# Six one-bank PSUM tiles for attention, and one-bank tiles for its projections and gates

## The chip, the cores and the metric

The kernel runs on one core of a Trainium2 chip. The metric is device time in microseconds (us) of one execution, given as the median of several runs. A core has TensorE (in the profile PE for its matmuls, PEld for loading their weights), VectorE (DVE), ScalarE (ACT), GpSimd (POOL) and SyncE (SP), which here issues most DMAs. TensorE writes its results to PSUM, and VectorE and ScalarE copy them to SBUF. PSUM is used here in units of one bank: 128 partitions by 512 float32 values, the most that one matmul of this kernel writes. There are eight banks.

## The reference, cut to what matters

One layer of a bidirectional encoder over 1024 tokens of width 1024. Its first part has two branches that share one input projection: windowed attention with grouped heads, and a state-space scan (SSD). Each branch is projected, gated by a sigmoid and merged; then come cross-attention and an MLP. The change concerns the windowed attention, and the gates that are computed beside it:

```python
proj = h @ w_in[i]
q = proj[..., :OFF_K].reshape(b, l, 16, 64)        # 16 heads of 64
k = proj[..., OFF_K:OFF_V].reshape(b, l, 4, 64)    # 4 key heads, each for 4 query heads
v = proj[..., OFF_V:OFF_Z].reshape(b, l, 4, 64)
gate_a, gate_b = ...                                # 1024 columns each
# per block of 128 queries: keys of this block and of both neighbours
s = einsum('bnqgrd,bnkgd->bngrqk', qb, kw) * 64 ** -0.5 + bias   # ALiBi, banded
m = max(max(s), sink); p = exp(s - m); denom = sum(p) + exp(sink - m)
o = einsum('bngrqk,bnkgd->bnqgrd', p / denom, vw)
merged = sigmoid(gate_a) * (attn @ w_attn_branch) + sigmoid(gate_b) * (ssd @ w_ssd_branch)
```

## The kernel before, in words

Phases follow one another: norms and small projections, the SSD scan (`ssd_phase`), attention (`attn_phase`), the merge (`merge_phase`), cross-attention and the MLP. In the SSD phase and from the merge on, the order of TensorE's instructions is the order in which they are written. In `attn_phase` it isn't: there the scheduler of the build orders every engine's instructions, by their place in the program among those that it holds to be ready, and that order is then fixed. So TensorE's order interleaves the steps below. In all phases waits are placed by data and by buffers: a tile of a pool with `bufs=n` takes the place of an earlier one, and waits until that one has been read.

Large products are made in three passes of high and low parts (`mm3`, lines 85, 89 and 90), so `gemm_fm` makes 24 matmuls for one block of 128 features by 512 tokens: 8 slices of the contraction by 3. The activations `kx.hT` (tile name kt) lie in two token halves. Weights are loaded by SP, split into whi (ACT, line 66) and wlo (POOL, line 69).

Before the change PSUM is shared out as follows in the SSD phase and in attention: the pool `pg` holds two tiles of two banks ([128, 1024], tag g), and the pool `pp` four tiles of one bank (tag p). The merge opens a pool of eight one-bank tiles in their place (line 1647).

Attention runs over four key heads kv. For each:

- For every second kv, keys of two heads are projected to a two-bank tile (`kps`, 48 matmuls), then copied to kh (ACT, lines 694 and 695) and to the rests kl (DVE, lines 696 and 697). The tags kh and kl have two buffers each, so keys of heads 2 and 3 need the buffers of heads 0 and 1.
- For the first kv, values are projected for all heads (`v_part`, tile vp, in the pool `pp`).
- Queries of two heads at a time are projected to a two-bank tile (`qps`, 48 matmuls; twice for each kv). ACT copies one head's half of the partitions (line 714), DVE computes the rest to the other half (line 715). The tag q has six buffers, of which a kv uses four.
- `scores(qb)` for each of eight query blocks: for each of four heads two matmuls to a one-bank tile sps (lines 732 and 733), then one DVE instruction that adds the bias, stores the sum to t and takes its minimum, nm (line 734). Then DVE and ACT compute the exponentials of t (line 740) and the denominators, and POOL scales t (line 745). The tag t4 has three buffers.
- `values(qb)`: for each of two or three key blocks, four transposes of t to a one-bank tile pt (line 755), copied by ACT to ph (line 758) and by DVE to the rest pl (line 759); then pairs of matmuls with ph and pl add up in a one-bank tile op (lines 764 and 765). ACT copies it in two halves, oa and ob (lines 768 and 769), POOL adds them, and SP stores the sum.
- The program makes `scores` two blocks ahead of `values`.
- After the last block of a kv come the gates of `ATT_GATES[kv]`: none, 11, 12, and 13 and 14. A gate is a two-bank tile gps of 48 matmuls, two ACT copies through a tanh (line 347), and two stores.

Since the order is by readiness, the matmuls of gates and of the next kv's keys and queries fill in between those of scores and values.

Of the kernel before, what the change touches and what calls it, by code (L numbers as in the profile page):

```python
# [7 lines left out]
F32 = mybir.dt.float32  # L8
F32R = mybir.dt.float32r
I32 = mybir.dt.int32  # L10
AF = mybir.ActivationFunctionType
ALU = mybir.AluOpType
AX = mybir.AxisListType
PSUM = bass.MemoryType.PSUM
DRAM = bass.MemoryType.DRAM

P = 128
S = 1024
# [74 lines left out]
def act_pair(act, k, sl=slice(None)):  # L93
    t = act[k // 4]
    return t[:, k % 4, 0, sl], t[:, k % 4, 1, sl]
# [6 lines left out]
def wsplit(w, nk=NK):  # L102
    hi = w[0].rearrange("p (k c) -> p k c", k=nk)
    lo = w[1].rearrange("p (k c) -> p k c", k=nk)
    return [(hi[:, k], lo[:, k]) for k in range(nk)]


def gemm_fm(kx, ps, w, act, first=True, last=True):

    ws = wsplit(w)  # L110
    for k in range(NK):
        mm3(kx, ps, ws[k], act_pair(act, k), first and k == 0, last and k == NK - 1)
# [224 lines left out]
def gate_block(kx, ins, dr, m, pool=None, pin=False):  # L337
    nc = kx.nc
    w = wload(kx, ins["wg"][m])
    ps = kx.pg.tile([P, S], F32, tag="g", name="gps")  # L340
    if pin:
        pin_next_matmul(kx)
    for h in range(2):
        gemm_fm(kx, ps[:, h * 512:(h + 1) * 512], w, kx.hT[h])
    gt = (pool or kx.tabp).tile([P, 2, 512], F32, tag="tab", bufs=1, name="gt")
    for h in range(2):
        nc.scalar.activation(gt[:, h], ps[:, h * 512:(h + 1) * 512], AF.Tanh, scale=0.5)
        (nc.sync if m in (7, 8) else nc.scalar).dma_start(dr.gt[m][h], gt[:, h])


def pin_next_matmul(kx):
    kx.pin = True
# [296 lines left out]
def attn_phase(kx, ins, dr):  # L649
    nc, tc = kx.nc, kx.tc  # L650
    V, A, G, PE = nc.vector, nc.scalar, nc.gpsimd, nc.tensor
    with tc.tile_pool(name="p2", bufs=1) as ap, tc.tile_pool(name="p2r", bufs=1, side="right") as aq:
# [30 lines left out]
        kd = {}  # L683
        for kv in range(4):
            if kv % 2 == 0:
                w = wload(kx, ins["wk"][kv // 2])
                ps = kx.pg.tile([P, S], F32, tag="g", name="kps")
                for h in range(2):
                    gemm_fm(kx, ps[:, h * 512:(h + 1) * 512], w, kx.hT[h])
                for s in range(2):  # L690
                    kh = aq.tile([P, S], F32R, tag="kh", bufs=2, name="kh")
                    kl = aq.tile([P, S], F32R, tag="kl", bufs=2, name="kl")
                    own, oth = slice(64 * s, 64 * s + 64), slice(64 - 64 * s, 128 - 64 * s)
                    A.activation(kh[own], ps[own], AF.Copy)
                    A.activation(kh[oth], ps[own], AF.Copy)
                    V.tensor_tensor(kl[own], ps[own], kh[own].bitcast(F32), ALU.subtract)
                    V.tensor_tensor(kl[oth], ps[own], kh[own].bitcast(F32), ALU.subtract)
                    kd[kv + s] = (kh, kl)
            if kv == 0:
                v_part()  # L700
            qs, bias = [], []
# [3 lines left out]
                bias.append(bt)  # L705
            for i in range(2):
                w = wload(kx, ins["wq"][2 * kv + i])
                ps = kx.pg.tile([P, S], F32, tag="g", name="qps")
                for h in range(2):
                    gemm_fm(kx, ps[:, h * 512:(h + 1) * 512], w, kx.hT[h])  # L710
                for s in range(2):
                    q = aq.tile([P, S], F32R, tag="q", bufs=6, name="q")
                    own, oth = slice(64 * s, 64 * s + 64), slice(64 - 64 * s, 128 - 64 * s)
                    A.activation(q[own], ps[own], AF.Copy, scale=-0.125)
                    V.scalar_tensor_tensor(q[oth], ps[own], -0.125, q[own].bitcast(F32), ALU.mult, ALU.subtract)
                    qs.append((q, own))
            kh, kl = kd[kv]
            def scores(qb):
                kb0, kb1 = max(qb - 1, 0), min(qb + 2, NT)
# [60 lines left out]
            for m in ATT_GATES[kv]:  # L780
                gate_block(kx, ins, dr, m)
# [821 lines left out]
@with_exitstack  # L1603
def hybrid_encoder(ctx, tc, ins, out, dbg=None):
    nc = tc.nc
    kx = Ctx()
    kx.nc, kx.tc = nc, tc
    kx.pin = False
    kx.w_bufs = 3
    kx.raw_bufs = 2  # L1610
    kx.cp = ctx.enter_context(tc.tile_pool(name="const", bufs=1))
    kx.wp = ctx.enter_context(tc.tile_pool(name="w", bufs=1))
    kx.mp = ctx.enter_context(tc.tile_pool(name="m", bufs=1))
    psum = ExitStack()
    kx.pg = psum.enter_context(tc.tile_pool(name="pg", bufs=2, space=PSUM))
    kx.pp = psum.enter_context(tc.tile_pool(name="pp", bufs=4, space=PSUM))
    dp = ctx.enter_context(tc.tile_pool(name="dram", bufs=1, space=DRAM))
    dr = Ctx()
    dr.cs = dp.tile([P, 512], F32, name="d_cs")
    dr.dec = dp.tile([P, 4], F32, name="d_dec")  # L1620
    dr.kx = dp.tile([P, 1024], F32, name="d_kx")
    dr.vx = dp.tile([P, 1024], F32, name="d_vx")
    dr.at = [[dp.tile([P, 4, 512], F32, name=f"d_at{k}_{h}") for h in range(2)] for k in range(2)]
    dr.y = [dp.tile([P, S], F32, name=f"d_y{k}") for k in range(16)]
    dr.gt = [[dp.tile([P, 512], F32, name=f"d_gt{k}_{h}") for h in range(2)] for k in range(16)]
    dr.x1 = [dp.tile([P, D], F32, name=f"d_x{k}") for k in range(4)]
    dr.u = [dp.tile([P, 1024], F32, name=f"d_u{k}") for k in range(32)]
    kx.dbg = dbg
    consts(kx)
    with tc.tile_pool(name="dtc", bufs=1) as dtc:  # L1630
        kx.coef = dtc.tile([P, 2, 4, 2, 32], F32, name="coef")
        kx.ebias = dtc.tile([P, 2, 4, 2, 32], F32, name="ebias")
        kx.ecs = dtc.tile([P, 2, 4, 2, 32], F32, name="ecs")
        kx.dec = dtc.tile([P, P, 4], F32, name="dec")
        with tc.tile_pool(name="conv", bufs=1) as kx.conv_pool:
            phase0(kx, ins, dr)
            ssd_phase(kx, ins, dr)
    with tc.tile_pool(name="tabp", bufs=1) as kx.tabp:
        attn_phase(kx, ins, dr)
        x1_low = ExitStack()  # L1640

        def x1_open():
            high = ctx.enter_context(tc.tile_pool(name="x1b", bufs=1, side="right", reuse_waits="tile"))
            return [x1_low.enter_context(tc.tile_pool(name="x1a", bufs=1, side="right", reuse_waits="tile")), high]

        psum.close()
        kx.pp = ctx.enter_context(tc.tile_pool(name="p8", bufs=8, space=PSUM, reuse_waits="tile"))
        h2T = merge_phase(kx, ins, dr, x1_open)
        ok, grow = cross_phase(kx, ins, dr, *h2T)
        with tc.manual_schedule(engines={mybir.EngineType.PE}):  # L1650
            down_phase(kx, ins, dr, up_phase(kx, ins, dr, ok, grow, x1_low), out)
    kx.dr = dr
    return kx
# [73 lines left out]
```

## Time and profile before

| | us |
|---|---|
| median of 3 runs | 2354.52 (2348.69 to 2355.77) |
| profiled execution | 2358.81 |
| its span, first to last instruction | 2357.0 |
| TensorE busy with matmuls | 2316.2 (98%) |
| TensorE busy loading weights | 1937.7 (82%) |
| DVE, ACT, POOL busy | 1623.7, 1155.2, 956.8 |

The granted TensorE clock was 0.997 of full speed. The keys' first matmul in attention starts at 909.65 us of the span, and the merge's first at 1236.91. In rows of the profile, L732 is line 732 of the kernel; `sps<-kh,q` is what an instruction writes and reads; x128 counts instructions. In a list of instructions the two first numbers are the start and the duration in us, and brackets hold the idle time of the engine before it and what ended it. A matmul's duration includes its way through the array, so durations of following matmuls overlap; how fast they follow is read from their starts.

### The profile page before, as it was taken

The page shows a single profiled execution, that of the slowest core. Times are in us where ns is not written, and L with a number is a line of the kernel's source. Part 1 is how long each engine was busy: PE and PEld are TensorE (multiplying, and loading weights), DVE is VectorE, ACT ScalarE, POOL GpSimd, SP SyncE. Part 2 cuts the span into 40 slices and gives each one's busy share as a digit, 9 for nine tenths or more (in the row PEclk, how much of TensorE's full clock was granted, in tenths as well). Part 3 has the DMA queues.
Part 4 walks back from the last instruction along what each step waited for, and adds up shares of the span by engine and source line. Part 5 has one row for each costly group of instructions (what it writes and reads, how often), then busy time and mean ns, then how long its engine had stood idle before and what let it go on. Part 6 is the DMA issues. An engine that isn't in the chain of part 4 may idle for free.

```text
span 2357.0 us, 32504 instructions
## 1 busy us (share of the span) xinstructions
PE 2316.2 (98%) x11876; PEld 1937.7 (82%) x11876; DVE 1623.7 (69%) x2539; ACT 1155.2 (49%) x2462; POOL 956.8 (41%) x891
## 2 busy tenths in 40 slices
PE   9999999999999999999999999999999999999998
PEld 7888898988889898877777888788977887788887
DVE  4777766677766664474568887975585456689984
ACT  4455655555555564586775442345453333134341
POOL 2355647565574653454540014215475444200010
PEclk9999999999999999999999999999999999999999
DMA  6223323232232322111136256202353345722301
GB/s 221 90 76 96 103 77 112 77 108 81 90 113 72 121 83 79 41 36 59 37 95 227 72 182 234 75 18 81 115 169 129 107 130 178 290 81 86 120 27 72
DMA packets 150036, 251.04 MB, mean 107 GB/s; under 512 B 11250, under 2 KB 86130, under 8 KB 149876
## 3 DMA queue, kind: packets, MB, share of 16 engines
q1 hardware_dynamic: 79264, 210.67, 26.3%
q10 hardware_dynamic: 70612, 38.29, 5.8%
q8 instruction: 94, 1.54, 0.3%
q14 instruction: 66, 0.54, 0.1%
HBM read 201.47 MB, written 47.45 MB: 106 GB/s over the span
## 4 chain that ended last, share of the span: by engine, by line
PE 79%; DVE 9%; DMA 3%; ACT 3%; issue 3%; POOL 2%; SPq 0%; POOLq 0%; ACTq 0%; DVEq 0%
PE dps L1497 10%; PE mps L1497 8%; PE pb L1292 6%; PE cps L90 4%; PE cps L85 4%; PE cps L89 4%; PE pc L1292 3%; PE zp L85 3%; PE zp L90 3%; PE zp L89 3%; PE cb L572 2%; PE yo L576 2%; PE gps L85 2%; PE gps L89 2%; PE gps L90 2%
## 5 line engine op out<-in xcount | busy, mean ns | idle before, releaser
L69 POOL TENSOR_TENSOR wlo<-raw,whi 128x1024 fp32r<-128x1024 f32 x104 | 255.6, 2458 | 408.2 <-ACT whi L66 379.9
L1497 PE MATMUL mps<-kt 128*128 128x512 f32 x1008 | 232.2, 391 | 4.9 <-DVE kt L1449 4.9
L1448 ACT ACTIVATE kt<-row 128x512 fp32r<-128x512 f32 x264 | 144.3, 619 | 187.1 <-PE dps L1497 83.0
L1497 PE MATMUL dps<-kt 128*128 128x512 f32 x1008 | 228.6, 389 | 0.0
L1497 PEld LDWEIGHTS mps<-kt 128*128 128x128 f32 x1008 | 189.7, 189 | 46.3 <-DVE kt L1449 7.0
L1497 PEld LDWEIGHTS dps<-kt 128*128 128x128 f32 x1008 | 189.2, 188 | 39.3
L85 PE MATMUL cps<-kt,whi 128*128 128x512 f32 x512 | 215.0, 420 | 0.0
L90 PE MATMUL cps<-kt,wlo 128*128 128x512 f32 x512 | 200.0, 391 | 0.0
L89 PE MATMUL cps<-kt,whi 128*128 128x512 f32 x512 | 199.3, 389 | 0.0
L66 ACT ACTIVATE whi<-raw 128x1024 fp32r<-128x1024 f32 x104 | 109.5, 1054 | 183.1 <-DMA raw<-in_wa_dram 42.1
L1449 DVE TENSOR_TENSOR kt<-row,kt 128x512 fp32r<-128x512 f32 x264 | 172.2, 700 | 3.8 <-ACT kt L1448 3.7
L124 POOL TENSOR_TENSOR rr<-rv,mhalf 128x1 f32<-128x1 f32 (+1 forms) x50 | 35.0, 701 | 235.8 <-DVE rv L122 229.8
L514 POOL TENSOR_TENSOR xl<-xs,xh 128x512 fp32r<-128x512 f32 (+1 forms) x64 | 86.3, 1350 | 103.5 <-ACT xh L513 79.0
L1238 POOL TENSOR_TENSOR wop<-w,wop 128x512 fp32r<-128x512 f32 x64 | 85.4, 1338 | 87.8 <-ACT wop L1237 79.1
L89 PEld LDWEIGHTS cps<-kt,whi 128*128 128x128 f32 x512 | 96.3, 188 | 25.4 <-issue 6.7
L85 PEld LDWEIGHTS cps<-kt,whi 128*128 128x128 f32 x512 | 96.3, 188 | 24.9 <-issue 6.0
L90 PEld LDWEIGHTS cps<-kt,wlo 128*128 128x128 f32 x512 | 96.1, 188 | 20.7
L550 ACT ACTIVATE eb<-rows,ebias 128x128 f32<-128x128 f32 x256 | 89.1, 392 | 35.4 <-POOL rows L542 35.4
L549 ACT ACTIVATE ef<-rows,ebias 128x128 f32<-128x128 f32 x256 | 90.5, 393 | 30.3 <-PE cb L572 27.8
L1177 POOL TENSOR_TENSOR wd<-row,wd 128x1024 fp32r<-128x1024 f32 x4 | 11.2, 2801 | 228.4 <-ACT wd L1176 228.4
L85 PE MATMUL gps<-kt,whi 128*128 128x512 f32 x240 | 102.2, 426 | 0.0
L745 POOL TENSOR_SCALAR t<-t,den 128x384 f32<-128x384 f32 (+1 forms) x128 | 69.2, 560 | 80.4 <-DVE den L743 68.5
(377 smaller groups left out, 6586.4 us busy)
## 6 DMA issues: line engine op xcount, KB each, us to landing
rows<-d_cs ACTq DMA_DIRECT2D x128, 256.0 KB, 4.0
raw<-in_wssd_dram SPq DMA_DIRECT2D x48, 512.0 KB, 3.8
raw<-in_wup_dram SPq DMA_DIRECT2D x40, 512.0 KB, 3.8
d_u<-c SPq DMA_DIRECT2D x64, 256.0 KB, 2.3
row<-in_wdn_dram SPq DMA_DIRECT2D x28, 512.0 KB, 6.7
row<-d_u SPq DMA_DIRECT2D x28, 512.0 KB, 6.7
x<-in_x_dram SPq DMA_DIRECT2D x16, 512.0 KB, 6.4
raw<-in_wg_dram SPq DMA_DIRECT2D x16, 512.0 KB, 3.7
```

The costliest lines, as they stand in the source:

```text
L66: steps = [nc.scalar.activation(hi, raw, AF.Copy)]
L69: steps.append((eng or nc.gpsimd).tensor_tensor(lo, raw, hi.bitcast(F32), ALU.subtract))
L85: i = mm(out, l[0], r[0], start=first, stop=False)
L89: mm(out, l[0], r[1], start=False, stop=False)
L90: mm(out, l[1], r[0], start=False, stop=last)
L514: G.tensor_tensor(xl[:, lo:hi], xf[:, lo:hi], xh[:, lo:hi].bitcast(F32), ALU.subtract)
L549: A.activation(ef[:, h], rows[:, 0, h], AF.Exp, bias=kx.ebias[:, b, j, 0, o:o + 1])
L550: A.activation(eb[:, h], rows[:, 1, h], AF.Exp, bias=kx.ebias[:, b, j, 1, o:o + 1])
L1292: self.kx.nc.tensor.matmul(ps, w[:, i, ks], act[:, k, j], start=start and k == 0 and m == 0, stop=k == 3 and m == 2, skip_group_check=True)
L1448: nc.scalar.activation(t[:, j, 0], src, AF.Copy)
L1449: nc.vector.tensor_tensor(t[:, j, 1], src, t[:, j, 0].bitcast(F32), ALU.subtract)
L1497: self.kx.nc.tensor.matmul(ps[t], lt[:, k, x, ts], rt[:, k, y], start=n in (1, 2, 5) and k == 0 and m == 0, stop=k == 3 and m == 2, skip_g ...
```

## The change

After the SSD phase the PSUM pools are closed, and two new ones are opened for attention: `pg2` with two tiles of one bank and `pp6` with six tiles of one bank. Both are opened with `reuse_waits="tile"`: a tile waits only for those users of the old pools that used its own bank. Scores, transposes, outputs and the value projection then take their tiles from six in place of four. Projections of keys and queries and the gates of this phase are made in halves of 512 tokens, each in a one-bank tile of its own, and each half is copied when its own matmuls are done. The copies of keys and queries are twice as many, each half as wide; those of gates are as many and as wide as before. No matmul is added or removed, and no DMA.

```diff
 def gate_block(kx, ins, dr, m, pool=None, pin=False):
...
-    ps = kx.pg.tile([P, S], F32, tag="g", name="gps")
...
-    for h in range(2):
-        gemm_fm(kx, ps[:, h * 512:(h + 1) * 512], w, kx.hT[h])
     gt = (pool or kx.tabp).tile([P, 2, 512], F32, tag="tab", bufs=1, name="gt")
     for h in range(2):
-        nc.scalar.activation(gt[:, h], ps[:, h * 512:(h + 1) * 512], AF.Tanh, scale=0.5)
+        ps = kx.pg.tile([P, 512], F32, tag="g", name="gps")
+        gemm_fm(kx, ps, w, kx.hT[h])
+        nc.scalar.activation(gt[:, h], ps, AF.Tanh, scale=0.5)
...
@@ attn_phase, keys
-                ps = kx.pg.tile([P, S], F32, tag="g", name="kps")
+                for s in range(2):
+                    kd[kv + s] = [aq.tile([P, S], F32R, tag=n, bufs=2, name=n) for n in ("kh", "kl")]
                 for h in range(2):
-                    gemm_fm(kx, ps[:, h * 512:(h + 1) * 512], w, kx.hT[h])
-                for s in range(2):
-                    kh = aq.tile([P, S], F32R, tag="kh", bufs=2, name="kh")
-                    kl = aq.tile([P, S], F32R, tag="kl", bufs=2, name="kl")
...
+                    ps = kx.pg.tile([P, 512], F32, tag="g", name="kps")
+                    gemm_fm(kx, ps, w, kx.hT[h])
+                    hs = slice(h * 512, (h + 1) * 512)
+                    for s in range(2):
+                        kh, kl = (t[:, hs] for t in kd[kv + s])
...
@@ attn_phase, queries
-                ps = kx.pg.tile([P, S], F32, tag="g", name="qps")
+                q2 = [aq.tile([P, S], F32R, tag="q", bufs=6, name="q") for _ in range(2)]
                 for h in range(2):
-                    gemm_fm(kx, ps[:, h * 512:(h + 1) * 512], w, kx.hT[h])
-                for s in range(2):
-                    q = aq.tile([P, S], F32R, tag="q", bufs=6, name="q")
...
+                    ps = kx.pg.tile([P, 512], F32, tag="g", name="qps")
+                    gemm_fm(kx, ps, w, kx.hT[h])
+                    for s in range(2):
+                        q = q2[s][:, h * 512:(h + 1) * 512]
...
+                qs += [(q2[s], slice(64 * s, 64 * s + 64)) for s in range(2)]
...
@@ hybrid_encoder, after ssd_phase
+    psum.close()
+    kx.pg = psum.enter_context(tc.tile_pool(name="pg2", bufs=2, space=PSUM, reuse_waits="tile"))
+    kx.pp = psum.enter_context(tc.tile_pool(name="pp6", bufs=6, space=PSUM, reuse_waits="tile"))
```

More of the change, by code (lines that the diff above doesn't have):

```diff
@@ L686, in attn_phase @@
                 w = wload(kx, ins["wk"][kv // 2])
-                ps = kx.pg.tile([P, S], F32, tag="g", name="kps")
+                for s in range(2):
+                    kd[kv + s] = [aq.tile([P, S], F32R, tag=n, bufs=2, name=n) for n in ("kh", "kl")]
                 for h in range(2):
-                    gemm_fm(kx, ps[:, h * 512:(h + 1) * 512], w, kx.hT[h])
-                for s in range(2):
-                    kh = aq.tile([P, S], F32R, tag="kh", bufs=2, name="kh")
-                    kl = aq.tile([P, S], F32R, tag="kl", bufs=2, name="kl")
[L693 to L698, printed above, removed]
+                    ps = kx.pg.tile([P, 512], F32, tag="g", name="kps")
[3 more added lines that the diff above has]
+                        kh, kl = (t[:, hs] for t in kd[kv + s])
+                        own, oth = slice(64 * s, 64 * s + 64), slice(64 - 64 * s, 128 - 64 * s)
+                        A.activation(kh[own], ps[own], AF.Copy)
+                        A.activation(kh[oth], ps[own], AF.Copy)
+                        V.tensor_tensor(kl[own], ps[own], kh[own].bitcast(F32), ALU.subtract)
+                        V.tensor_tensor(kl[oth], ps[own], kh[own].bitcast(F32), ALU.subtract)
             if kv == 0:
@@ L707, in attn_phase @@
                 w = wload(kx, ins["wq"][2 * kv + i])
-                ps = kx.pg.tile([P, S], F32, tag="g", name="qps")
+                q2 = [aq.tile([P, S], F32R, tag="q", bufs=6, name="q") for _ in range(2)]
                 for h in range(2):
-                    gemm_fm(kx, ps[:, h * 512:(h + 1) * 512], w, kx.hT[h])
-                for s in range(2):
-                    q = aq.tile([P, S], F32R, tag="q", bufs=6, name="q")
[L713 to L716, printed above, removed]
+                    ps = kx.pg.tile([P, 512], F32, tag="g", name="qps")
+                    gemm_fm(kx, ps, w, kx.hT[h])
+                    for s in range(2):
+                        q = q2[s][:, h * 512:(h + 1) * 512]
+                        own, oth = slice(64 * s, 64 * s + 64), slice(64 - 64 * s, 128 - 64 * s)
+                        A.activation(q[own], ps[own], AF.Copy, scale=-0.125)
+                        V.scalar_tensor_tensor(q[oth], ps[own], -0.125, q[own].bitcast(F32), ALU.mult, ALU.subtract)
+                qs += [(q2[s], slice(64 * s, 64 * s + 64)) for s in range(2)]
             kh, kl = kd[kv]
```

## The prediction

> **What bounds the kernel now.** I read the page's busy shares first, then cut the attention phase (909.65 to 1236.91 us) into stages, then read who waits for whom there, and last one steady stage in order of time.
>
> ```profile
> PE 2316.2 (98%) x11876; PEld 1937.7 (82%) x11876; DVE 1623.7 (69%) x2539; ACT 1155.2 (49%) x2462; POOL 956.8 (41%) x891
> ```
>
> TensorE is the bound, but 98% is matmul time with overlaps: it doesn't show the gaps. So I compare starts with the spacing of undisturbed matmuls. Next: stretches, with busy us (and instructions) of PE, PEld, DVE, ACT, POOL; the third row holds the matmuls and copies of qps alone.
>
> ```profile
> 1055.53:1061.73 6.20, 6.11 (x33) 4.72 (x33) 4.79 (x16) 5.22 (x16) 3.55 (x5) 1.00 0.10 24
> 992.00:1000.00 8.00, 8.00 (x43) 6.10 (x42) 6.55 (x18) 7.92 (x21) 5.53 (x9) 1.00 0.08 18
> 1085.40:1107.30 21.90, 21.84 (x96) 17.85 (x96) 2.44 (x2) 2.04 (x2) 1.00 0.19 61
> ```
>
> The third row is TensorE alone with a projection: 21.90/96 = 0.228 us for a 512-column matmul. The first is one steady attention stage (scores of one query block, values of an earlier one), 6.20 us long, in which no engine is full: ACT 5.22, DVE 4.79. Now the timeline of TensorE, weight loads, ACT and DVE around that stage.
>
> ```profile
> 1144.92 1.47 PE L755 MATMUL pt<-ident,t 128*128 128x128 f32 x12
> 1146.15 0.48 PE L90 MATMUL qps<-kt,wlo 128*128 128x512 f32 x1
> 1054.16 0.19 PEld L732 LDWEIGHTS sps<-kh,q 128*128 128x128 f32 x1 [0.39 <-DVE nm L734]
> 1055.53 0.52 PE L755 MATMUL pt<-ident,t 128*128 128x128 f32 x3
> 1057.13 0.60 PE L755 MATMUL pt<-ident,t 128*128 128x128 f32 x4
> 1057.33 1.28 DVE L759 TENSOR_TENSOR pl<-pt,ph 128x512 fp32r<-128x512 f32 x2
> 1057.46 0.59 ACT L768 ACTIVATE oa<-op 64x512 f32<-64x512 f32 x1
> 1058.06 0.50 PE L764 MATMUL op<-ph,vhl 128*128 128x512 f32 x1
> 1058.07 0.60 ACT L769 ACTIVATE ob<-op 64x512 f32<-64x512 f32 x1
> 1059.09 0.34 PE L732 MATMUL sps<-kh,q 128*128 128x384 f32 x1
> 1059.26 0.34 PE L733 MATMUL sps<-kl,q 128*128 128x384 f32 x1
> 1059.75 0.56 DVE L734 CUSTOM_DVE_ANT_0 t<-sps,bias 128x384 f32<-128x384 f32 x1 [1.15 <-PE sps L733]
> 1062.17 0.66 DVE L759 TENSOR_TENSOR pl<-pt,ph 128x512 fp32r<-128x512 f32 x1
> ```
>
> Spacings: a transpose (1146.15 - 1144.92)/12 = 0.103 us, a score matmul 1059.26 - 1059.09 = 0.17. The stage's 33 matmuls are 12 transposes, 8 scores, 6 for the output and so 7 of a projection or gate that fills in: 12 x 0.103 + 8 x 0.17 + 13 x 0.228 = 5.56 us. TensorE thus loses 6.20 - 5.56 = **0.64 us per stage**, 20.5 us over 32 stages (4 key heads x 8 blocks).
>
> Why the stage isn't shorter: count the four PSUM banks that sps, pt and op share. The third transpose bank is written at 1057.13 and read last by DVE until 1062.83: 5.7 us. An output bank is opened at 1058.06, so the one before it a stage earlier, at 1051.86, and that one is copied from 1057.46 to 1058.67: 6.8 us. The first two transpose banks are written from 1055.53 and read until 1058.61, each open some 2.5 us; four scores take some 1.2 us each (1059.09 to the end of the reduction at 1060.31). Together 5.7 + 6.8 + 5.0 + 4.8 = 22.3 bank-us, of 4 x 6.20 = 24.8: the four banks are 90% taken. The third score's weight load at 1054.16 waits for the reduction of an earlier score, and DVE sits idle 1.15 us for scores that have no bank. The weight loads' waits in the whole phase (total us, times, longest):
>
> ```profile
> PEld sps L732 <- DVE nm L734: 7.2, 23, 0.4
> PEld op L764 <- ACT ph L758: 6.9, 15, 0.7
> PEld pt L755 <- POOL t L745: 5.2, 16, 0.5
> PEld op L764 <- DVE pl L759: 4.7, 12, 0.5
> PEld op L765 <- DVE pl L759: 4.4, 12, 1.0
> PEld pt L755 <- issue: 3.7, 11, 0.6
> PEld sps L732 <- DVE q L715: 2.2, 6, 0.6
> PEld sps L732 <- ACT ob L769: 1.7, 3, 0.6
> PEld mps L85 <- ACT gt L347: 1.2, 1, 1.2
> ```
>
> Rows 1 and 8 are waits for a bank. I count rows 3 and 6 so too: the transposes follow the scores directly, and start when a reduction frees a bank; this is inferred. That makes 7.2 + 5.2 + 3.7 + 1.7 = 17.8. Waits for data are 6.9 + 4.7 + 4.4 = 16.0, and 2.2 are for a projection's copy. In all 36.0.
>
> **The change, part by part.**
>
> *Six banks for sps, pt, op instead of four.* The need of 22.3 bank-us becomes 22.3/6 = 3.7 us per stage and no longer binds; next in line are TensorE's 5.56 and ACT's 5.22. Of the 20.5 us lost, the bank waits' share is 17.8/36.0: **-10.1 us**. Ends: 0 (every wait comes back as another) and -20.5 (all waits go). I take the share, since only those waits have the removed cause.
>
> *Waits for data.* A shorter stage leaves ACT and DVE less slack, and the output matmuls wait for both already (16.0). I add **+1.5**, near the lower end of 0 to +10.1, since DVE's 1.15 us of idle time per stage covers the first of it.
>
> *Projections in two one-bank halves.* The matmuls stay as many. The copies of q and k double in number at half the width:
>
> ```profile
> L714 ACT ACTIVATE q<-qps 64x1024 fp32r<-64x1024 f32 x16 | 16.3, 1019 | 6.9 <-DVE q L715 6.8
> L768 ACT ACTIVATE oa<-op 64x512 f32<-64x512 f32 x32 | 18.8, 587 | 14.9 <-PE op L765 14.8
> L715 DVE SCALAR_TENSOR_TENSOR q<-qps,q 64x1024 fp32r<-64x1024 f32 x16 | 19.6, 1222 | 20.7 <-ACT q L714 20.4
> L759 DVE TENSOR_TENSOR pl<-pt,ph 128x512 fp32r<-128x512 f32 x88 | 57.2, 678 | 19.5 <-ACT ph L758 19.4
> L696 DVE TENSOR_TENSOR kl<-kps,kh 64x1024 fp32r<-64x1024 f32 x4 | 4.9, 1222 | 11.4 <-ACT kh L695 11.4
> ```
> ```profile
> L694 ACT ACTIVATE kh<-kps x4: 1001/1022/1023, 923.3 to 1091.5; 64x1024 fp32r<-64x1024 f32 x4
> ```
>
> ACT: 16 q copies and 8 of k (two lines of 4) grow from about 1020 to 2 x 587 = 1174 ns: 24 x 0.154 = 3.7 us. DVE: 24 x (2 x 0.678 - 1.222) = 3.2 us. On the path I put **0**: ACT is at 5.22 of 6.20 and, in the dense stretch, at 2.04 of 21.90 with q copies. Without that cover it is the 3.7, the upper end; the stretch 992 to 1000 (ACT 7.92 of 8) shows that cover can fail. In return the first half is copied while the second is multiplied, and scores of early blocks need only the first half: the 2.2 of waits for q go, by the same share 20.5 x 2.2/36.0 = **-1.2** (0 to -2.2). Here a rule speaks against the change: the Trainium skill's "Perfetto Trace Analysis", section "Optimizing Scalar/DVE Operations", says that each instruction on these engines pays a fixed data-access overhead, and that fewer, larger ones help where the engine is saturated. By its PSUM figures (about 51 ns on ScalarE, 125 on DVE) the estimate would be 24 x 51 = 1.2 and 24 x 125 = 3.0 us; the trace has 154 and 134 ns each, and the sum goes by the trace.
>
> *The gates* copy each half as it is done; the copies are as many and as wide as before. The last gate and the start of the phase:
>
> ```profile
> 1235.77 1.08 ACT L347 ACTIVATE gt<-gps 128x512 f32<-128x512 f32 x2 [1.06 <-PE gps L90]
> 1236.91 0.50 PE L85 MATMUL mps<-kt,whi 128*128 128x512 f32 x1 [0.89 <-ACT gt L347]
> 909.65 0.58 PE L85 MATMUL kps<-kt,whi 128*128 128x512 f32 x1
> 909.70 1.08 ACT L450 ACTIVATE gt<-gps 128x512 f32<-128x512 f32 x2
> 914.30 0.33 PE L606 MATMUL yt<-ident,yz 128*128 128x128 f32 x1 [0.86 <-ACT yz L598]
> ```
>
> At the end the merge's first matmul idles 0.89 us for both copies of the gate; the first half's bank will be free long before: **-0.9** (0 to -0.9). The stores of the gates stay on their queues; no transfer is added or moved.
>
> *The new pools ahead of attention.* Tiles wait per bank, not for the old pools as a whole. The first key projection starts at 909.65; if its bank was the previous gate's, it waits until 910.78: **+1.1**. At best 0. At worst the whole old pool must drain, and the key matmuls that now fill until the last transposes at 914.30 move behind them: +4.6. I take the wait for one bank, since that is what the pools declare.
>
> **Sum:** -10.1 + 1.5 + 0 - 1.2 - 0.9 + 1.1 = -9.6 us. It stands against this execution's 2358.8 (span 2357.0 and 1.8 around it): 2349.2. The median of the three runs is 2354.5, 4.3 lower, so I forecast **2345** as the median after. About 0.3% (7.1 us) is what a measurement of this kernel can tell from no change.
>
> **Rivals.**
>
> *Waits for data re-form (no change).* The instructions of each engine stand in a fixed order; if output matmuls wait for ph and pl as long as scores waited for banks, the 10.1 come back: -1.2 - 0.9 + 1.1 = -1.0, 2353.5. For it: 16.0 of 36.0 are such waits already. Against: DVE's 1.15 us idle is caused by banks. A measured case on this side, from the Trainium skill's "TensorE: Matmul & The Clock Gate", section "HAM oscillation — how this bites in real kernels": a matmul kernel gained nothing further from double-buffered PSUM. No run here shows it, and here the banks are 90% taken.
>
> *ACT is the bound (no change).* If ACT's 5.22 with its order sets the stage, the 10.1 don't come and the 3.7 lie on the path: +3.7 + 1.1 - 0.9 = +3.9, 2358.4. This is what the rule on larger instructions would give. For it: 7.92 of 8 us; against it: 16% idle in the steady stage.
>
> *DVE takes scores first (slower).* With banks free, scores of the next block come sooner, and their reductions (0.56 + 0.08 us each) may be queued ahead of the pl that the output waits for. Two of them ahead cost 1.28 per stage, less the 0.32 won (10.1/32): +0.96 in half of the stages, -0.32 in the rest: 16 x 0.64 = +10.2, 2365. From a delay of 0.32 us per stage the change loses. Against it: DVE is at 4.79 of 6.20.
>
> *The filling matmuls run dry (slower).* Two one-bank tiles hold 48 finished matmuls where two double tiles held 96. The second head's k copies wait for k buffers that the scores hold to the end of the stretch below. Its matmuls, first of the key tile, then of the gate:
>
> ```profile
> 1026.90:1069.20 42.30, 5.78 (x18) 3.15 (x19) 0.00 (x0) 0.00 (x0) 1.00 0.14 42
> 1026.90:1069.20 42.30, 14.89 (x48) 8.75 (x48) 1.09 (x2) 1.00 0.14 42
> ```
>
> 66 were used, and 96 can now be issued before both banks are stuck: 30 x 0.228 = 6.8 us to spare. If the order uses them up early, a stage loses its 7 x 0.228 = 1.6 us; ten such stages are 16, less the 9.6: +6.4, 2361. It decides from six stages on.
>
> **How the numbers follow.** Forecast 0.60, waits re-form 0.14, ACT 0.08, DVE 0.11, fillers 0.07. So faster 0.60, same 0.22, slower 0.18. The likeliest alone runs from 2334 (all 20.5 lost us won: -20.5 - 0.9 + 1.1 = -20.3) to 2347. The range is 2333 to 2361: it takes in both cases of no change, reaches to the fillers' price, and leaves out DVE's and half of the fillers'.
>
> **What would show it.** Right: the wait of sps for nm is near nothing, the steady stage near 5.8 us, DVE's idle time before its first reduction gone, spacings unchanged. Wrong: the waits of op for pl or ph above 16 us by the same amount; ACT full in steady stages; stages without projection matmuls; a gap between 909 and 915.

## The result, and the profile after

The changed kernel takes 2348.4 us (median of 22 runs, 2345.4 to 2353.2), the kernel before 2352.3 us (22 runs, 2348.1 to 2357.9): ratio 0.9985 with a 95% interval of 0.9980 to 0.9991. A second set of runs gave 0.9980 (0.9972 to 0.9989). So it is faster, but by 3.9 us instead of the forecast 9.6, which lies inside the 0.3% that the prediction called no change.

To compare the attention phase I use its length from the first matmul of kps to the first of mps. Every kernel below issues the same matmuls in it; at their undisturbed spacings they take 294.4 us (294.6 with 0.228, 0.174, 0.120 and 0.103 us for the 848, 192, 256 and 360 matmuls of 512, 384, 256 and 128 columns; differences between kernels don't hang on this figure). What the phase takes beyond that is called **lost time** of TensorE. In two executions of the change the phase took 322.72 and 322.70 us, so it repeats better than whole executions, which spread over 8 to 10 us; the kernel before and the same with its pools reopened differ more, 327.26 and 326.08. The timeline rows of the two matmuls that bound the phase after:

```profile
908.61 0.50 PE L85 MATMUL kps<-kt,whi 128*128 128x512 f32 x1 [0.83 <-ACT gt L449]
...
1231.32 0.39 PE L85 MATMUL mps<-kt,whi 128*128 128x512 f32 x1
```

The phase is 1231.32 - 908.61 = 322.71 us, before 1236.91 - 909.65 = 327.26: it lost 28.3 instead of 32.9 us. The weight loads' waits in the phase (total us, times, longest) changed like this:

```profile
PEld op L765 <- ACT ph L759: 8.8, 19, 0.9
PEld pt L756 <- POOL t L746: 6.2, 20, 0.6
PEld op L766 <- DVE pl L760: 5.6, 12, 1.4
PEld sps L733 <- DVE nm L735: 3.2, 7, 1.2
PEld qps L85 <- issue: 1.8, 1, 1.8
PEld kps L85 <- ACT gt L449: 1.2, 1, 1.2
```

The wait of scores for a bank (sps for nm) fell from 7.2 to 3.2, the waits for q and for ob are gone, and the outputs' waits for ph and pl fell from 16.0 to 14.4. The transposes' wait for t, which POOL scales, rose from 5.2 to 6.2. DVE's own waits, the first row before, the others after:

```profile
DVE t L734 <- PE sps L733: 50.6, 49, 6.3
```
```profile
DVE den L743 <- ACT t L741: 29.4, 19, 3.4
DVE t L735 <- PE sps L734: 13.6, 11, 3.0
```

DVE now rarely waits for scores (13.6 us instead of 50.6). It waits for ACT instead: 29.4 us for the exponentials in front of den (16.3 before), and 40.9 in front of its part of q (20.4 before). What became of the stages is seen in the last key head, by the copies of its first and its sixth output, before and after:

```profile
1195.98 0.60 ACT L769 ACTIVATE ob<-op 64x512 f32<-64x512 f32 x1
...
1229.57 0.59 ACT L769 ACTIVATE ob<-op 64x512 f32<-64x512 f32 x1
```
```profile
1189.85 0.60 ACT L770 ACTIVATE ob<-op 64x512 f32<-64x512 f32 x1
...
1218.66 0.59 ACT L770 ACTIVATE ob<-op 64x512 f32<-64x512 f32 x1
```

The first five stages last (1229.57 - 1195.98)/5 = 6.7 us before and (1218.66 - 1189.85)/5 = 5.8 after, and the last output is copied at 1224.57 instead of 1237.35, 12.8 us earlier. But the merge starts only 5.6 us earlier: between 1224.60 and 1231.30 TensorE is busy without a gap, with gate matmuls that used to fill the stages. **A shorter stage is no gain by itself. TensorE's work only moves, and the gain is the gaps that close.**

### The profile page after: what moved, and what is told of

It is laid out like the page before. It is cut to its first block, busy times and chain, and to the rows that moved or that the text cites. A ratio compares the mean times of both kernels' runs of the same rounds, so it can differ in the third digit from the quotient of the medians.

```text
span 2345.7 us, 32548 instructions
## 1 busy us (share of the span) xinstructions
PE 2307.1 (98%) x11876; PEld 1941.4 (83%) x11876; DVE 1620.7 (69%) x2563; ACT 1157.8 (49%) x2486; POOL 959.2 (41%) x891
## 4 chain that ended last, share of the span: by engine, by line
PE 81%; DVE 8%; ACT 4%; issue 3%; POOL 3%; DMA 1%; POOLq 0%; ACTq 0%; DVEq 0%
PE dps L1498 10%; PE mps L1498 9%; PE pb L1293 6%; PE cps L90 5%; PE cps L85 5%; PE cps L89 4%; PE pc L1293 3%; PE zp L85 2%; PE zp L90 2%; PE zp L89 2%; PE cb L571 2%; PE yo L575 2%; PE gps L89 2%; PE gps L85 2%; PE gps L90 2%
## 5 line engine op out<-in xcount | busy, mean ns | idle before, releaser
L89 PEld LDWEIGHTS cps<-kt,whi 128*128 128x128 f32 x512 | 96.3, 188 | 25.3 <-issue 6.7
L548 ACT ACTIVATE ef<-rows,ebias 128x128 f32<-128x128 f32 x256 | 90.6, 393 | 33.9 <-PE cb L571 31.7
L1178 POOL TENSOR_TENSOR wd<-row,wd 128x1024 fp32r<-128x1024 f32 x4 | 12.6, 3169 | 227.6 <-ACT wd L1177 225.7
L1293 PE MATMUL pb<-kt,wop 128*128 128x512 f32 x384 | 93.1, 391 | 2.3 <-ACT c L1347 2.3
```

The source lines that it names most:

```text
L89: mm(out, l[0], r[1], start=False, stop=False)
L548: A.activation(ef[:, h], rows[:, 0, h], AF.Exp, bias=kx.ebias[:, b, j, 0, o:o + 1])
L1293: self.kx.nc.tensor.matmul(ps, w[:, i, ks], act[:, k, j], start=start and k == 0 and m == 0, stop=k == 3 and m == 2, skip_group_check=True)
```

## The experiments

Ratios are to the kernel before on the same chip; lost is the lost time of the profiled execution in attention. The last column sums what nm, es and den (DVE's three instructions on 128x4 elements per block, 96 in all) take beyond 0.16 us each, from groups like those shown further down.

| kernel | banks for sps/pt/op, projections | ratio (95%) | lost, us | nm, es, den, us over |
|---|---|---|---|---|
| before | 4, two double tiles | 1 | 32.9 | 12.0 |
| pools closed and reopened | 4, two double | 1.0007 (0.9998-1.0015) | 31.7 | 12.1 |
| six and one double tile | 6, one double | 1.0314 (1.0300-1.0328) | 103.7 | 5.1 |
| halves, four banks | 4, four | 1.0034 (1.0021-1.0048) | 35.9 | 13.5 |
| halves, four banks, two empty | 4, two | 1.0071 (1.0058-1.0083) | 36.5 | 13.4 |
| the same, snk in PSUM | 4, two | 0.9981 (0.9972-0.9990) | 26.9 | 1.8 |
| q alone in halves | 4, two double | 1.0042 (1.0030-1.0054) | 41.7 | 12.0 |
| keys and gates alone in halves | 4, two double | 1.0013 (1.0005-1.0022) | 35.1 | 9.9 |
| five banks, one empty | 5, two | 0.9956 (0.9942-0.9970) | 21.8 | 3.4 |
| five and three | 5, three | 0.9968 (0.9957-0.9979) | 21.6 | 3.5 |
| five and three, four k buffers | 5, three | 0.9953 (0.9940-0.9966) | 21.6 | 3.5 |
| the change | 6, two | 0.9985 (0.9980-0.9991) | 28.3 | 9.7 |
| the change, eight q buffers | 6, two | 0.9983 (0.9974-0.9992) | 28.4 | 9.9 |

### The change with four banks, two left empty

```diff
-    kx.pp = psum.enter_context(tc.tile_pool(name="pp6", bufs=6, space=PSUM, reuse_waits="tile"))
+    kx.pp = psum.enter_context(tc.tile_pool(name="pp6", bufs=4, space=PSUM, reuse_waits="tile"))
```

> The changed kernel with four banks instead of six for sps, pt and op (two banks stay empty); the halves stay. Theory (the banks made the gain): the waits of sps for nm are back near 7 us, TensorE's lost time in the phase near 33 us, and the time is that of the kernel before, ratio 0.999 to 1.001. Rival (copying in halves made the gain): like the changed kernel, ratio 0.998 to 0.999, waits for nm near 3 us.

Lost time 36.5, ratio 1.0071: without the two banks the change is slower than the kernel before. The theory had the waits for banks right (7.3 us) and the time wrong: it held that halves cost nothing. In this form, four to six banks are worth 36.5 - 28.3 = 8.2 us of the phase. Of the weight loads' waits, the scores' for banks fall by 4.1 us (7.3 to 3.2) and the outputs' for ph and pl by 11.0 (25.4 to 14.4).

### The halves alone

```diff
-    kx.pg = psum.enter_context(tc.tile_pool(name="pg2", bufs=2, space=PSUM, reuse_waits="tile"))
-    kx.pp = psum.enter_context(tc.tile_pool(name="pp6", bufs=6, space=PSUM, reuse_waits="tile"))
+    kx.pg = psum.enter_context(tc.tile_pool(name="pg2", bufs=4, space=PSUM, reuse_waits="tile"))
+    kx.pp = psum.enter_context(tc.tile_pool(name="pp6", bufs=4, space=PSUM, reuse_waits="tile"))
```

> The halves alone: four one-bank tiles for projections and gates, four for sps, pt and op. Theory (the banks made the gain): no gain, ratio 0.999 to 1.001, as with four banks the chain of a key head is as long as before (about 53 us from the first minimum to the last output copy). Rival (halves made it): 0.998 or better, since here nothing was taken from the projections.

This has the same banks as the kernel before, only cut in halves, and it is slower by 0.34% (0.21 to 0.48), which neither the theory nor the rival had expected. The phase is 330.33 - 327.26 = 3.1 us longer; the ratio means 8 us, and what makes up the rest is open. The weight loads' waits for its outputs:

```profile
PEld op L765 <- ACT ph L759: 16.6, 29, 2.8
PEld op L766 <- DVE pl L760: 8.0, 22, 1.7
PEld sps L733 <- DVE nm L735: 7.1, 24, 0.4
```

Scores wait for banks as long as before (7.1 and 7.2), but outputs wait 25.3 us for ph and pl (with a third row of 0.7) where it was 16.0. The order of instructions on each engine is fixed when the kernel is built, and with the halves another order is built. What in this order makes ph and pl late is seen in "DVE behind POOL".

The kernel with two empty banks has nearly this order (25 of the phase's 1657 matmuls stand elsewhere, the other engines' orders are the same) and nearly this phase, 0.5 us longer. That its ratio is higher goes with the clock: over its runs the mean granted clock is 0.9956, here 0.9983. If the time follows the clock, 0.0027 of 2360 us makes 6.4 of the 8.1 us between the means of the two; this is an estimate. Its profiled execution, at 0.997, took 2362.5 us, and the one here, at 0.998, 2362.3. Why the clock was lower in its other runs stays open, since no trace was taken of them.

### Six banks without the halves

```diff
+    psum.close()
+    kx.pg = psum.enter_context(tc.tile_pool(name="pg2", bufs=1, space=PSUM, reuse_waits="tile"))
+    kx.pp = psum.enter_context(tc.tile_pool(name="pp6", bufs=6, space=PSUM, reuse_waits="tile"))
     with tc.tile_pool(name="tabp", bufs=1) as kx.tabp:
```

> The banks alone: six banks for sps, pt and op, and one undivided two-bank tile for projections and gates. Theory: the waits for banks go as in the changed kernel, but each projection must wait for the copies of the one ahead (2 x (1.02 + 1.22) = 4.5 us) where nothing else fills; some four such places, +18, less the 4 won: ratio 1.004 to 1.008. This would show that halves are what pays for the two banks. Rival (halves make the gain by themselves): here too slower, but with waits of sps for nm still near 7 us.

It is 3.1% slower, several times what was expected. With one double tile, the next projection cannot start while the last one is being copied:

```profile
PEld sps L732 <- DVE q L715: 32.7, 12, 3.6
PEld qps L85 <- issue: 20.6, 5, 10.4
```

These waits also come with a lower clock: 0.985 over the execution. So the halves are the price of the two banks, and not an improvement that stands beside them.

### The pools closed and reopened

```diff
+    psum.close()
+    kx.pg = psum.enter_context(tc.tile_pool(name="pg2", bufs=2, space=PSUM, reuse_waits="tile"))
+    kx.pp = psum.enter_context(tc.tile_pool(name="pp6", bufs=4, space=PSUM, reuse_waits="tile"))
     with tc.tile_pool(name="tabp", bufs=1) as kx.tabp:
```

> The kernel before with its PSUM pools closed and opened again in the same sizes ahead of attention. Theory (tiles wait for their own bank alone): the key projection starts up to 1.2 us later, ratio 1.000 to 1.001. Rival (the old pools are drained first): a gap of TensorE between 909 and 915, +4.6 us, ratio 1.002.

1.0007, with 1 inside the interval: nothing that can be measured. The trace has the wait of kps for gt, 1.2 us, and no gap of 4.6, so the old pools are not drained first.

### q alone, and keys and gates alone, in halves

The kernel before with only this part of the change's diff, and then with its parts for keys and gates alone:

```diff
-                ps = kx.pg.tile([P, S], F32, tag="g", name="qps")
+                q2 = [aq.tile([P, S], F32R, tag="q", bufs=6, name="q") for _ in range(2)]
                 for h in range(2):
-                    gemm_fm(kx, ps[:, h * 512:(h + 1) * 512], w, kx.hT[h])
+                    ps = kx.pg.tile([P, 512], F32, tag="g", name="qps")
+                    gemm_fm(kx, ps, w, kx.hT[h])
 ...
```
```diff
-                ps = kx.pg.tile([P, S], F32, tag="g", name="kps")
+                    ps = kx.pg.tile([P, 512], F32, tag="g", name="kps")
 ...
-    ps = kx.pg.tile([P, S], F32, tag="g", name="gps")
+        ps = kx.pg.tile([P, 512], F32, tag="g", name="gps")
 ...
```

> The kernel before with only the query projections in halves (tiles of one bank, each in a slot of two; four banks for sps, pt and op). Theory (halves hand all four heads' scores over at once, and with four banks the build then finds an order in which stages take 7 to 9 us instead of 6.2): this part alone costs what the halves alone cost, ratio 1.003 to 1.007, waits of op for ph near 16 us. Rival (each added copy costs by itself, 0.15 us on ACT): two thirds of that (16 of 24 added copies), 1.002 to 1.0045, with stages of 6.2 us and no longer waits for ph.

> The kernel before with only the keys and the gates in halves. Theory (order): no change, ratio 0.999 to 1.001, stages of 6.2 us. Rival (added copies): a third of the cost, 1.001 to 1.002, and waits of the projections for k copies.

q alone costs 0.42%, keys and gates alone 0.13% (0.05 to 0.22). The first ratio lies where the theory had it, but not for its reason: outputs wait 6.6 us for ph, where it expected some 16. Most of the 8.8 us that q alone loses more than the kernel before is a second cost of a bad order. One qps matmul waits for a double tile that the k copies hold, and the clock drops behind it (columns of the second fence as in the prediction's stretches: length, busy and count of PE, PEld, DVE, ACT, POOL, granted clock, DMA share, GB/s):

```profile
1097.10 0.77 PE L85 MATMUL qps<-kt,whi 128*128 128x512 f32 x1 [4.72 <-DVE kl L697]
```
```profile
1060.00:1080.00 20.00, 19.60 (x107) 14.88 (x106) 11.78 (x35) 16.71 (x42) 10.21 (x15) 1.00 0.18 53
1080.00:1100.00 20.00, 15.28 (x61) 11.98 (x60) 6.96 (x7) 10.09 (x14) 7.33 (x4) 0.87 0.21 66
1100.00:1120.00 20.00, 20.00 (x91) 16.55 (x90) 6.33 (x18) 5.69 (x9) 4.81 (x2) 0.96 0.09 27
```

From 1097.10 to 1101.83 eleven matmuls take 4.73 us, where at the 0.227 of those that follow they would take 2.50: 2.2 us on top of the gap of 4.72. With keys and gates alone no projection waits for a copy of k, against its rival; there the outputs wait 21.6 us for ph and pl instead of 16.0.

### More q buffers

```diff
-                q2 = [aq.tile([P, S], F32R, tag="q", bufs=6, name="q") for _ in range(2)]
+                q2 = [aq.tile([P, S], F32R, tag="q", bufs=8, name="q") for _ in range(2)]
```

> The changed kernel with eight buffers for q instead of six. If the q buffers hold the projection's banks at the change from key head 0 to 1 (the fourth half was multiplied only from 1018.8, after the first scores of head 1), key heads 0 and 1 lose some 4 us less: ratio 0.996 to 0.998 against the kernel before. If waits for ph and pl set it: as the changed kernel, 0.998 to 0.999.

The order built is the same on every engine and the lost time is the same within 0.1 us. My guess that q's buffers hold the first two heads back fell.

### Three and five

```diff
-    kx.pg = psum.enter_context(tc.tile_pool(name="pg2", bufs=2, space=PSUM, reuse_waits="tile"))
-    kx.pp = psum.enter_context(tc.tile_pool(name="pp6", bufs=6, space=PSUM, reuse_waits="tile"))
+    kx.pg = psum.enter_context(tc.tile_pool(name="pg2", bufs=3, space=PSUM, reuse_waits="tile"))
+    kx.pp = psum.enter_context(tc.tile_pool(name="pp6", bufs=5, space=PSUM, reuse_waits="tile"))
```

> The changed kernel with three banks for projections and gates and five for sps, pt and op. If the bank that projections lost is what was given back (TensorE waited 1.8 us for k copies at 1083, and key heads 0 and 1 lost 15.7 us together against 15.2 before), the third bank takes this away: ratio 0.996 to 0.998. If the sixth bank for scores is what counts: between four and six, 1.000 to 1.003.

0.9968, faster than the change, with 21.6 us lost instead of 28.3. Whether the third projection bank or the missing sixth does it, the next three runs tell.

### Five banks, one empty; three and five with more k buffers; the change again

The first edit is to the change, the second to three and five; the third kernel is the change as it is.

```diff
-    kx.pp = psum.enter_context(tc.tile_pool(name="pp6", bufs=6, space=PSUM, reuse_waits="tile"))
+    kx.pp = psum.enter_context(tc.tile_pool(name="pp6", bufs=5, space=PSUM, reuse_waits="tile"))
```
```diff
-                    kd[kv + s] = [aq.tile([P, S], F32R, tag=n, bufs=2, name=n) for n in ("kh", "kl")]
+                    kd[kv + s] = [aq.tile([P, S], F32R, tag=n, bufs=4, name=n) for n in ("kh", "kl")]
```

> Changed kernel with five banks instead of six for scores, transposes and outputs (pool pp6 with bufs=5), projections still in two one-bank tiles; one bank stays empty. It tells whether the gain of three plus five banks is due to the third projection bank. Theory 'banks by the piece': TensorE's lost time in attention lies between that with four (36.5 us) and six (28.3 us), about 32, the ratio to the kernel before about 1.003, and the first scores of the second key head come as early as in the changed kernel, with a quarter of their q still missing. Rival 'five is enough, six is one too many' (the scores run too far ahead with six): lost time about 22, ratio about 0.997, as with three plus five. Rival 'four to five gives all': about 28, ratio 0.9985.

> Three one-bank tiles for projections and gates, five for scores, transposes and outputs, and four k buffers instead of two (kh and kl), so that the second pair's key copies wait for no buffer. Theory 'k buffers still hold a projection': the second key head loses about 1.5 us less, ratio about 0.996. Rival 'they hold nothing once there are three projection banks': within 1 us of three plus five with two k buffers (0.9968), lost time 21 to 22 us.

> The changed kernel unchanged, on the same chip as the two others, so that three plus five banks can be set against two plus six in one set of runs: ratio 0.9985 to the kernel before if the first measurement holds; above 0.9995 the change is no change at all. The difference to three plus five should be 0.0015 to 0.002.

Five banks and one **empty** give 0.9956, three and five with four k buffers 0.9953: the best ratios, and their intervals lie below that of the change in the same set of runs (0.9972 to 0.9989). The rival "five is enough, six is one too many" named the lost time. In the phase the order of instructions of five and one empty is the same on every engine as in three and five, with two k buffers or four, and the lost time is within 0.2 us: neither the third projection bank nor the k buffers gain anything. The waits with five banks and one empty:

```profile
PEld sps L733 <- DVE nm L735: 5.8, 22, 0.4
PEld pt L756 <- POOL t L746: 5.2, 16, 0.5
PEld op L765 <- ACT ph L759: 4.5, 17, 0.5
PEld op L766 <- DVE pl L760: 2.5, 10, 0.4
```

With five banks, scores wait longer for a bank than with six (5.8 and 3.2), and yet the kernel is faster, since its outputs wait 7.0 us instead of 14.4. So what six lose against five isn't a matter of too few banks.

### DVE behind POOL

What makes ph and pl late? In the change with four banks, around one of the long waits of an output (rows of POOL, DVE, ACT and TensorE from its timeline):

```profile
1140.96 2.38 POOL L69 TENSOR_TENSOR wlo<-raw,whi 128x1024 fp32r<-128x1024 f32 x1
1141.88 1.48 DVE L737 TENSOR_TENSOR nm<-nm,snk 128x4 f32<-128x4 f32 x1
1143.30 1.28 POOL L771 TENSOR_TENSOR oa<-oa,ob 64x512 f32<-64x512 f32 x1
1143.39 1.21 DVE L738 TENSOR_TENSOR es<-nm,snk 128x4 f32<-128x4 f32 x1
1144.64 0.20 ACT L739 ACTIVATE es<-es 128x4 f32<-128x4 f32 x1 [2.32 <-DVE es L738]
...
1147.26 1.58 ACT L759 ACTIVATE ph<-pt 128x512 fp32r<-128x512 f32 x3
1147.91 0.50 PE L765 MATMUL op<-ph,vhl 128*128 128x512 f32 x1 [2.35 <-ACT ph L759]
```

A minimum over 128x4 elements takes 1.48 us, and it ends at 1143.36, when POOL's instruction ends (1143.34). The next one starts just after POOL's next and ends with it (1144.60 and 1144.58). ACT idles 2.32 us for es, then takes the four exponentials of this block, and only then copies the three ph that had been queued behind them; the output waits 2.35 us. In the changed kernel the largest loss at an output has the same form:

```profile
1060.40 1.27 POOL L771 TENSOR_TENSOR oa<-oa,ob 64x512 f32<-64x512 f32 x1
1060.49 1.20 DVE L738 TENSOR_TENSOR es<-nm,snk 128x4 f32<-128x4 f32 x1
1061.62 0.68 DVE L760 TENSOR_TENSOR pl<-pt,ph 128x512 fp32r<-128x512 f32 x1
1062.35 0.50 PE L766 MATMUL op<-pl,vhl 128*128 128x512 f32 x1 [1.20 <-DVE pl L760]
```

Its ph is there at 1060.02, but pl stands behind es, and es behind POOL. This is so throughout: of the 96 instructions nm, es and den, those that start while a POOL instruction still has more than 0.15 us to run (38 before, 26 in the change) all end within 0.03 us of its end; the others take at most 0.17 us. DVE's instructions with an input in PSUM don't show it: pl takes 0.68 us beside a POOL instruction and without one. The other runs have five exceptions, which took 0.15 us; they started within 0.08 us of POOL's instruction. The profile counts this standstill as busy time, so no row of waits shows it. To take it away, DVE's second input of nm and es is read in PSUM, in one of the two empty banks:

```diff
         V.tensor_scalar(snk[:, 1], snk[:, 0], -1.0, None, ALU.mult)
+        snp = kx.ps1.tile([P, 2, 16], F32, tag="snp", name="snp"); V.tensor_copy(snp, snk)
 ...
-                V.tensor_tensor(nm, nm, snk[:, 1, 4 * kv:4 * kv + 4], ALU.min)
-                V.tensor_tensor(es, nm, snk[:, 0, 4 * kv:4 * kv + 4], ALU.add)
+                V.tensor_tensor(nm, nm, snp[:, 1, 4 * kv:4 * kv + 4], ALU.min)
+                V.tensor_tensor(es, nm, snp[:, 0, 4 * kv:4 * kv + 4], ALU.add)
 ...
+    kx.ps1 = psum.enter_context(tc.tile_pool(name="ps1", bufs=1, space=PSUM, reuse_waits="tile"))
```

> Changed kernel with four banks for scores, transposes and outputs, as before, and in one of the two empty banks a copy of snk, which DVE's two small instructions per block (nm, es) read there instead of in SBUF. In the four-bank kernel's trace each of these instructions that starts while a POOL instruction runs ends when POOL's ends (26 of 26 for nm and es), 12.9 us beyond their usual 0.16 us in all. Theory 'DVE stands still behind POOL': with one input in PSUM they end after 0.2 us, the waits of output matmuls for pl and ph shrink, TensorE's lost time in attention falls from 36.5 to 24 to 30 us, and the ratio from 1.0071 to 1.003 or less. Rival 'four banks bind': lost time stays within 2 us of 36.5, ratio 1.006 to 1.008, whatever DVE does. Rival 'the order of the instructions decides': it changes a little here too, so a difference under 3 us tells nothing.

The groups (busy us, mean ns of one; idle time before them) with four banks and snk in SBUF, then with snk in PSUM, then those of the change:

```profile
L737 DVE TENSOR_TENSOR nm<-nm,snk 128x4 f32<-128x4 f32 x32 | 12.8, 400 | 0.9
L738 DVE TENSOR_TENSOR es<-nm,snk 128x4 f32<-128x4 f32 x32 | 10.3, 321 | 0.8
```
```profile
L737 DVE TENSOR_TENSOR nm<-nm,snp 128x4 f32<-128x4 f32 x32 | 5.0, 156 | 0.9
L738 DVE TENSOR_TENSOR es<-nm,snp 128x4 f32<-128x4 f32 x32 | 5.0, 155 | 0.7
```
```profile
L743 DVE TENSOR_TENSOR den<-den,es 128x4 f32<-128x4 f32 x32 | 10.1, 315 | 29.7 <-ACT t L741 29.4
L737 DVE TENSOR_TENSOR nm<-nm,snk 128x4 f32<-128x4 f32 x32 | 8.5, 265 | 0.5
L738 DVE TENSOR_TENSOR es<-nm,snk 128x4 f32<-128x4 f32 x32 | 6.5, 205 | 0.2
```

The last column of the table above comes from such groups: for the change 10.1 + 8.5 + 6.5 - 96 x 0.16 = 9.7 us. With snk in PSUM, nm and es take 156 and 155 ns whatever POOL does. Lost time falls from 36.5 to 26.9 us and the ratio from 1.0071 to 0.9981: **four banks without most of this standstill are as fast as six with it**. The fall of the ratio is 21 us, more than the 9.6 of the phase; part of that goes with the lower clock of the kernel with snk in SBUF (0.9956 over its runs, here 0.9978). The waits of this kernel:

```profile
PEld op L765 <- ACT ph L759: 10.4, 22, 0.9
PEld sps L733 <- DVE nm L735: 7.1, 26, 0.4
PEld pt L756 <- POOL t L746: 5.7, 16, 0.6
PEld op L766 <- DVE pl L760: 5.0, 20, 0.6
```

The scores still wait 7.1 us for a bank, as with snk in SBUF (7.3); the outputs' waits for ph and pl fell from 25.4 to 15.4. What of that is idle time of TensorE itself, with snk in SBUF and in PSUM:

```profile
PE op L765 <- ACT ph L759: 7.1, 11, 2.4
PE op L766 <- DVE pl L760: 1.8, 3, 1.3
```
```profile
PE op L765 <- ACT ph L759: 2.8, 10, 0.5
PE op L766 <- DVE pl L760: 0.6, 3, 0.2
```

Three places make up most of the 8.9 us in the first: 1.32 at 1007.95, 2.33 at 1065.79 and 2.35 at 1147.91, in all 6.0. At each of them nm has just stood behind a wlo and es behind an oa of POOL. With snk in PSUM no output idles TensorE for more than 0.5 us. The order of instructions changed with this edit too: some 290 of the 1657 matmuls and about a tenth of DVE's and ACT's instructions stand elsewhere. So of the 9.6 us, some 6 are seen at the places where the standstill was, and for the rest the new order is not ruled out. A difference of that size was what the theory named, and the rival that only banks count had said under 2.

## Why the prediction came out as it did, step by step

The chance for "faster by over 0.3%" was 0.60, and the result is inside the 0.3%: the likeliest case gave 2345, the measurement 2348.4. The sign and the range held, and the size was 40% of what was forecast. The base was small, too: the steady stage's 0.64 us gave 20.5 for the 32 stages, where the phase before lost 32.9.

**Six banks for four: -10.1, with +1.5 for data, so -8.6.** The two kernels in halves give -8.2 in the phase. The sum is right, by luck, and its reason only in part. Six banks did take more than half of the scores' waits away (7.2 to 3.2 us), and the outputs' waits did not grow. But the share of bank waits was no measure of what banks cost. The 5.2 us of transposes for POOL's t, counted as a bank wait by inference, stayed with five banks (5.2) and with six (6.2): it is a wait for data. Without it the share is 12.6/36.0, and the term -7.2. Five banks give -14.7 and the sixth gives 6.5 back; and taking DVE's standstill away, with four banks, gives -9.6. What is left between four banks without the standstill and five, with 1.8 and 3.4 us of it, is 26.9 - 21.8 = 5.1 us: this is the nearest that the runs come to the price of the banks by themselves, and the orders differ there as well. The count of 22.3 of 24.8 bank-us was not tested; but it holds some of the standstill too: in the stage that was counted, es takes 0.52 us at 1056.88, and pl stands behind it until 1057.33.

**Projections in halves: 0 on the path, -1.2 for q, and -0.9 for the gates. The 0 is the step that failed.** With four banks, where it stands alone, the phase is 3.1 (four projection banks) or 3.6 us (two) longer, not 2.1 shorter. The groups of the copies:

```profile
L716 DVE SCALAR_TENSOR_TENSOR q<-qps,q 64x512 fp32r<-64x512 f32 x32 | 22.0, 689 | 41.5 <-ACT q L715 40.9
L715 ACT ACTIVATE q<-qps 64x512 fp32r<-64x512 f32 x32 | 19.0, 593 | 25.1 <-PE qps L90 14.3 <-DVE q L716 10.5
```

They last what was worked out: 593 ns against 587 and 689 against 678, so ACT has 2.7 and DVE 2.4 us more for q. The wait of sps for q is gone as well. But the 0 on the path was argued from the room that ACT and DVE have, and not from their order: with another order, the outputs wait 25.3 instead of 16.0 us. In that order TensorE idles at three outputs for 1.3, 2.4 and 2.4 us, where the kernel before has only 0.8 at one; they are the places at which es stands behind POOL, and with snk in PSUM the same halves with four banks have a phase 6.0 us shorter than before. The upper end of 3.7 that the prediction kept for the case without cover happens to fit; its cause, the copies lying on the path, is not what the trace shows. The rule of the Trainium skill's "Perfetto Trace Analysis", section "Optimizing Scalar/DVE Operations", that larger instructions help where the engine is saturated, has the right sign here and not the reason. By their durations a split costs 167 ns (2 x 593 - 1019) on ScalarE and 156 (2 x 689 - 1222) on VectorE. But copies that follow one another overlap: the three ph at 1147.26 last 1.58 us together and 597 ns each, which would make 1.79. So these 167 and 156, and the 154 and 134 that the prediction's 3.7 and 3.2 rest on, are upper bounds of what a split takes of the engine's time. The PSUM figures of that section of the Trainium skill, about 51 and 125 ns, are engine-busy times, so the durations don't contradict them.

**The gates' end, -0.9, and the wait for the old gate's bank, +1.1.** Both right: the mps row at 1231.32 has no wait, and the weight load of kps waits 1.2 for gt (TensorE idles 0.83).

**The sum.** In the profiled executions: halves +3.6, banks -8.2, kps's wait +1.2, together -3.4. The medians show -3.9. The two profiled executions lie 11.3 us apart in span, and 5.7 of that is behind the phase (1120.1 us before, 1114.4 after). No run shows that this is the change's doing: the kernel with its pools closed and reopened, which loses 31.7 us in attention, has 1115.8 there. The same goes for the merge's mps, whose matmuls idle 4.9 us before and 1.6 after, but 2.8 with the pools reopened and 2.6 in the second execution of the change.

**The rivals.** "Waits for data re-form" named the result's size (2353.5 forecast, no change) but not its cause: those waits fell. "DVE takes scores first" had the right place: pl does stand behind a later block's es in the changed kernel. It put the price on the reductions (0.64 each), where es alone took 1.20 at that place because of POOL. "ACT is the bound" did not set the time, though its sign of being wrong came near: in the five stages of the last key head ACT is busy for 25.72 of 28.81 us (26.48 of 33.59 before), and for 5.68 of 5.80 in the stretch from 1200.00. With five banks the same copies are made and the phase is 6.5 us shorter, so ACT's work alone is not what holds six. "The filling matmuls run dry" did not happen: between 908.61 and 1231.32 the longest wait of a projection or gate is 1.8 us. The counterexample from the Trainium skill's "TensorE: Matmul & The Clock Gate", section "HAM oscillation — how this bites in real kernels", in which double buffering in PSUM gave nothing further, fits from five banks to six and does not fit from four to five.

**What stays open.** Whether six banks with snk in PSUM, or five, would gain more was not tried: six leave no bank for it, and with five only 3.4 us of the standstill are left, most of it at den, which that edit doesn't touch. Why the build's order with six banks meets POOL so much more often in the second key head is not settled. From one head's first scores to the next head's, six banks lose 6.0, 9.7, 5.6 and 5.6 us, the last up to the merge, and five 5.2, 5.7, 4.6 and 4.8; the standstill is 2.2, 5.0, 1.2 and 1.2 us with six and 0.8, 0.9, 0.9 and 0.9 with five. In the second head the two go together (4.0 and 4.1 us); in the last two heads 1.8 us of loss stand against 0.6. That the standstill makes most of the 6.5 us between six and five is argued from this, and no run shows it by itself.

## What to carry to other kernels

Before a wait is put down to a resource, look at the durations of the small instructions on the way to it: one of usually 0.16 us that takes 1.2 at times is a wait that the profile counts as work. Where the order of instructions is built from the buffers' number, a change of buffers is a change of order: measure the number next to it too (here five banks, with one left empty, were faster than six), and make one run with the new shapes but the old number. And a stage that gets shorter gains only the gaps that it closes, since the matmuls that filled it come later.

## What was not expected of the hardware

**DVE stands still behind POOL when both of its inputs are in SBUF.** In the kernels before and after and with four banks, nm, es and den took up to 1.48 us instead of 0.16 when a POOL instruction was running, and ended with it; with one input in PSUM, nm and es took 0.16 us beside a running POOL. The Trainium skill's "SBUF — State Buffer", section "Who interferes with whom", states that a DVE instruction with two SBUF inputs contends with a GpSimd instruction that reads SBUF, and that the order of issue decides which of two blocks. The traces agree with the first part, in 64 of 64 cases of the kernels before and after; the second is not tested here.

**A gap of TensorE is followed by a lower granted clock.** In q alone in halves, 4.7 us without a matmul stand in a stretch at 0.87, with 0.96 in the next (the rows above), where the stretch ahead has 1.00. So this gap of 4.72 us cost 2.2 us more than its length.
